# Two tile users regrouped by engine, the output projection's forms loaded in their stored layout, and its first half accumulated into the residual by transfers

## The chip, the cores and the metric

The kernel runs on one core of one Trainium2 chip. The metric is the device time of one execution in microseconds, the median of several executions. For the kernel before it is 2371.23 us (three runs, 2368.53 to 2372.38). Engines are called PE (TensorE, matmuls), DVE (VectorE), ACT (ScalarE), POOL (GpSimd, here mostly a queue that issues transfers) and SP (SyncE, a queue that issues transfers).

## The reference, cut to what matters

Two layers on a sequence of 512 tokens with 2048 features, all in 32-bit floats: forgetting attention (16 heads of 128), then retention (8 heads, keys of 256, values of 512). Each has one input projection, a gate, one output projection, a residual and a layer norm.

```python
def fox_branch(x, w_in, b_f, q_gain, k_gain, w_out):
    ...
    q = rms_norm(heads(q), q_gain)
    k = rms_norm(heads(k), k_gain)
    ...
    y = o * jax.nn.silu(gate)
    return jnp.einsum('bse,ed->bsd', y, w_out)

def retention_branch(x, w_in, w_out):
    ...
    o = group_norm_heads(o).reshape(B, S, RET_V_WIDTH).astype(gate.dtype)
    y = o * jax.nn.silu(gate)
    return jnp.einsum('bse,ed->bsd', y, w_out)

def reference(...):
    h = x
    for i in range(DEPTH):
        ...
        h = layer_norm(DEEPNORM_ALPHA * h + y, ln_gain[i], ln_bias[i])
    return h
```

The retention layer's output projection sums over 4096 features (8 heads of 512). The kernel does it in two halves of 2048 features, heads 0 to 3 and heads 4 to 7, whose results are added to the residual `DEEPNORM_ALPHA * h`.

## The kernel before, in words

**Matmuls.** A 32-bit product is made of three passes on split operands: every operand `t` is split into a rounded part `h` (ACT, L325) and the rest `l = t - h` (DVE, L326), and `mm3` issues `h*h`, `h*l` and `l*h` (L330, L331, L332). The large projections are `Unit`s, products of two 2x2 block matrices done with seven block products instead of eight (Strassen's way): each takes "forms" of the activations (`a11`, `a12`, `a22` and the sums `s1` to `s4`) and blocks of weights, some of which are sums too (`w_q`, DVE L595). The block results are combined in tiles called `kept` and in a buffer called `room`, and a finished quarter (m, n) of a unit's output goes to a function `sink`.

**Stages**, by the trace's lines: the first layer's projections and attention up to 835 us; its output projection with the layer norm and the transposes for the next layer from 835 to 1030 us; the eight retention heads up to about 2080 us; the second layer's output projection up to the end. That projection consists of units 14 and 15 (first four heads, left and right half of the output columns) and units 16 and 17 (last four heads).

**Order.** A planner (`Order`) writes the program block by block. Beside the matmul blocks there are tasks (Python generators); each `yield need(...)` names the DVE and ACT time that the next step costs, the buffers it takes and a condition, and the step is put into the program once the planner's debt of DVE and ACT leaves room. Each engine runs its instructions in the order written. SP issues the loads of weights, of stored forms (`y_raw`) and of the residual (`z_in`), in that one order; POOL issues the stores and the accumulating transfers. `tmp` is a ring of four buffers of 128x512, `mmp` a ring of two PSUM tiles for transposes and small products.

**What the change touches.**

- `to_parts` (L1099 to L1105), called 32 times between 144 and 799 us: it takes one `mmp` tile of transposed queries and keys, and for each of two pairs of columns ACT writes the scaled `qk_h` (L1102) and DVE the rest `qk_l` (L1103). Read and written by turns: ACT, DVE, ACT, DVE.
- `to_columns` (L1528 to L1592), the layer norm's transposes: sixteen times, PE transposes four 128x128 blocks into an `mmp` tile (L1567), and four copies with gain and bias bring them into a shared tile (called `raw` in the profile): j = 0 on ACT (L1585), j = 1 on DVE (L1583), j = 2 and 3 on ACT.
- `give_forms` (L842 to L846): when a retention head is done, ACT makes `y` and its negative `ny` (L1839, L1840) and POOL stores or accumulates them into the forms of the output projection in DRAM (`y_a` and `y_s` in the profile). The DRAM layout is 128 x 2 x 8 x 128. `given[1]` counts the heads so far.
- `fetch_forms` (L866 to L893): SP reads these forms back (L880) into `y_raw` in the layout 128 x 8 x 256, with a transfer for each of two halves of tokens and two halves of features, so a partition's row is four runs of 128 floats; then `split_form` splits them.
- `add_half` (L1890 to L1905), the sink of units 14 and 15: the residual's 16 blocks of 128x512 (`z_res`) are read back into the `tmp` ring by SP (`z_in`, L1474), DVE adds the finished quarter (L1898), and POOL stores the sum as `z_half` (L1899). Units 16 and 17 read `z_half` the same way.
- The tiles with finished quarters are freed by `done()`: (0,0), (0,1) and (1,1) lie in `kept` tiles or `room`, (1,0) still lies in PSUM (`acc`).

Of the kernel before, what the change touches and what calls it, by code (L numbers as in the profile page):

```python
# [11 lines left out]
F32 = mybir.dt.float32  # L12
# [5 lines left out]
P = 128  # L18
# [232 lines left out]
def trunk(ctx: ExitStack, tc: tile.TileContext, xq, x, fb_f, columns, wf_in, narrow, wide, ln_g, ln_b, rot, decay,  # L251
# [9 lines left out]
    def f32(t):  # L261
        return t.bitcast(F32)
# [571 lines left out]
           for f in (("a11", "a12", "a21", "a22") if i == 0 else FORM.values())} for i in range(3)]  # L834
    z_norm = [dram.tile([P, D], F32, name=f"z_norm{s}") for s in range(ST)]
    z_res = {(s, c): dram.tile([P, 512], F32, name=f"z_res{s}{c}") for s in range(ST) for c in range(4)}
    z_half = {(s, c): dram.tile([P, 512], F32, name=f"z_half{s}{c}") for s in range(ST) for c in range(4)}


    given = [0, 0]  # L840
# [25 lines left out]
    def fetch_forms(i, names):  # L866

        at = {}

        def loads():  # L870
            for n in names:
                if n not in VIA:
                    yield need(g0=1)
                    take("g0")
                t = pool.tile([P, 8, 256], F32, name="y_raw", tag=home[VIA[n]][0] if n in VIA else "g0")
                passing.add(VIA.get(n))
                for c in (0, 4):
                    yield need(wait=2, until=lambda: given[1] >= 4 * i)
                    for e in range(2):
                        nc.sync.dma_start(t[:, c:c + 4, e * P:(e + 1) * P], yf[i][n][:, e, c:c + 4])  # L880
                    at[n, c] = t, o.now

        spawn(loads(), 0)
        for n in names:
            for c in (0, 4):
                yield need(dve=1.14, act=0.97,
                           until=lambda: n not in passing and (n, c) in at and o.now - at[n, c][1] >= 4)
                if c == 0:
                    new_form(n)
                split_form(n, at[n, c][0][:, c:c + 4], c, c + 4)  # L890
            passing.discard(VIA.get(n))
            if n not in VIA:
                give("g0")  # L893
# [98 lines left out]
    class Pair:  # L992
# [88 lines left out]
        def normed(self):  # L1081

            yield need(until=lambda: self.have == 4 and fox["norms"] == self.i)
            raw = [self.raw[s // 2][:, s % 2] for s in range(ST)]
            r = self.ss
            yield need(dve=1.2)
            yield from rsqrt_steps(*[r.rearrange("p a b -> p (a b)")] * 2, 4 * ST, 1.0 / P, QK_EPS)
            scaled = {}
            for s in range(ST):
                yield need(dve=0.6, wait=0)  # L1090
                scaled[s] = o.due
                v = raw[s].rearrange("p (h d) -> p h d", h=4)
                nc.vector.tensor_mul(v, v, r[:, s, :, None].to_broadcast([P, 4, P]))
            yield need(until=lambda: all(free[t] for t in self.tags))
            for t in self.tags:
                take(t)
            self.qk = sb8("qk_h", self.tags[0], F32R), sb8("qk_l", self.tags[1], F32R)

            def to_parts(t, s):  # L1099
                for i, gain in ((0, gq), (2, gk)):  # L1100
                    h, l = (p[:, i:i + 2, s * P:(s + 1) * P] for p in self.qk)
                    nc.scalar.activation(h, t[:, i:i + 2], AF.Copy, scale=gain)  # L1102
                    nc.vector.scalar_tensor_tensor(l, t[:, i:i + 2], gain, f32(h), op0=ALU.mult, op1=ALU.subtract)  # L1103
                self.due = o.due
                give("mmp")  # L1105

            t, s, last = {}, ST if self.quick else 0, None
            for q in range(ST if self.quick else 0):
                yield need(act=0.75, dve=0.7, pe=0.45, wait=1 - q % 2, mmp=1, until=lambda: o.soon(scaled[q]))
                t[q] = by4(mmp())  # L1110
                for h in range(4):
                    nc.tensor.transpose(t[q][:, h], raw[q][:, h * P:(h + 1) * P], ident)
                to_parts(t[q], q)
            can = lambda: s < ST and free["mmp"] and o.soon(scaled[s])
            while s < ST or last is not None:
                yield need(act=0.75, dve=0.7, pe=0.45, until=lambda: last is not None or can())
                new = None
                if can():
                    new = s
                    t[s] = by4(mmp())  # L1120
                    for h in range(4):
                        nc.tensor.transpose(t[s][:, h], raw[s][:, h * P:(h + 1) * P], ident)
                    s += 1
                if last is not None:
                    to_parts(t[last], last)
                last = new
            give("in0")
            give("in1")
            fox["emptied"] = self.i + 1
            yield need()  # L1130
            fox["norms"] = self.i + 1
# [396 lines left out]
    def to_columns(m):  # L1528
# [28 lines left out]
        while i < 8 or last is not None or made:  # L1557
# [17 lines left out]
            if last is not None:  # L1575
                s, c = turns[last]
                es = slice(s % 2 * P, (s % 2 + 1) * P)
                d = aq[f"{m + 1}{c // 2 + 1}"][:, c % 2 * 4:c % 2 * 4 + 4, es]
                for j in range(4):
                    k = c * 4 + j  # L1580
                    g, b = cols[:, 2 + k:3 + k], cols[:, 2 + KT + k:3 + KT + k]
                    if j == 1:
                        nc.vector.tensor_scalar(d[:, j], ps[last][:, j], g, b, op0=ALU.mult, op1=ALU.add)  # L1583
                    else:
                        nc.scalar.activation(d[:, j], ps[last][:, j], AF.Identity, scale=g, bias=b)  # L1585
                give("mmp")
                if m == 0:
                    made.append(last)
                elif s % 2:
                    there.add((f"2{c // 2 + 1}", c % 2))  # L1590
# [296 lines left out]
                      then={**then, "p4": lambda h=h, last=last: (spawn(h.retain()), last())})  # L1887


    def add_half(u, held):  # L1890
        got, steps = loads_of(lambda s, c: z_res[s, c], u, "order", held)

        def sink(m, n, tile, done):
            def add():
                for e in range(2):
                    yield need(dve=0.6, until=lambda: (m, n, e) in got and o.now - got[m, n, e][1] >= 2)
                    t, _ = got.pop((m, n, e))
                    nc.vector.tensor_add(t, t, tile[:, e])  # L1898
                    nc.gpsimd.dma_start(z_half[2 * m + e, 2 * u + n], t)  # L1899
                    give("tmp", 3)  # L1900
                done()

            spawn(add(), 0)

        return sink, steps  # L1905

    sink, steps = add_half(0, 2)
    Unit(wide, 14, sink, u2="in1", p1="y0").run(then={"p6": lambda s=steps: spawn(s(), 1)})
    sink, steps = add_half(1, 2)
    Unit(wide, 15, sink, u2="k2").run(leaves=True, then={0: lambda s=steps: spawn(s(), 1), **fetch_while(2)})  # L1910

    gb = []

# [55 lines left out]
            else:  # L1969
                nc.gpsimd.dma_start(out[s * P:(s + 1) * P, cs], z, accum_op=ALU.add)  # L1970

    half = lambda s, c: z_half[s, c]
    spawn(join_room(), 0)
    sink, steps = add_z(0, 1, half, "order")
    Unit(wide, 16, sink, u2="k2").run(then={0: lambda s=steps: spawn(s(), 1)})
# [56 lines left out]
```

## Time and profile before

| | before |
|---|---|
| median of three runs | 2371.23 us |
| profiled execution, whole | 2373.73 us |
| its span from the first to the last instruction | 2372.0 us |
| mean granted TensorE clock | 0.993 |
| busy share of the span: PE, DVE, ACT, POOL | 97%, 80%, 51%, 7% |
| moved by transfers | 477.36 MB |

The span leaves out 1.73 us of the profiled execution. The busy share of PE is an average over stages; a table by stage, the waits and the transfers stand with the prediction. In rows that group instructions, the columns are: line, engine, operation, output and inputs, shapes, count, then busy time and mean ns of one, then the idle time of the engine just before them and what ended it.

### The profile page before, as it was taken

How to read it: one execution, taken by the hardware profiler on the slowest of the kernel's cores; microseconds unless marked ns; L12 is line 12 of the kernel's file. 1: busy time of each engine (PE TensorE's matmuls, PEld its weight loads, DVE VectorE, ACT ScalarE, POOL GpSimd, SP SyncE). 2: the span in 40 equal slices, each digit the busy share in tenths (PEclk: the TensorE clock that was granted, in tenths of full speed). 3: DMA queues.
4: the chain of work that ended last, by engine and by line, in shares of the span. 5: the costliest groups of instructions: out<-in, count | busy, mean ns of one | idle time of the engine just before them, and what ended most of it. 6: DMA issues, size and time to landing. Idle time of an engine off the chain costs nothing.

```text
span 2372.0 us, 32919 instructions
## 1 busy us (share of the span) xinstructions
PE 2307.9 (97%) x12424; PEld 1975.0 (83%) x12424; DVE 1892.5 (80%) x2477; ACT 1213.4 (51%) x1762; POOL 165.7 (7%) x256
## 2 busy tenths in 40 slices
PE   9999999999999999999999999999999999999995
PEld 9878778879899778888889898988888898787784
DVE  5887787787765656689889888888988889987877
ACT  4546556556555534565444545354545445554533
POOL 0000000000000000010100101010101000011002
PEclk9999999999999999999999999999999999999998
DMA  6356455455544456684685857575756659679778
GB/s 225 123 199 198 160 187 187 154 181 184 195 151 155 139 199 241 225 186 157 207 263 211 249 174 222 197 203 186 218 186 209 204 171 274 209 256 295 234 247 190
DMA packets 186350, 477.36 MB, mean 201 GB/s; under 512 B 18224, under 2 KB 63424, under 8 KB 185680
## 3 DMA queue, kind: packets, MB, share of 16 engines
q1 hardware_dynamic: 160288, 399.48, 50.3%
q0 software_dynamic: 25904, 75.78, 12.7%
q8 instruction: 97, 1.59, 0.3%
q14 instruction: 61, 0.50, 0.1%
HBM read 415.39 MB, written 64.00 MB: 202 GB/s over the span
## 4 chain that ended last, share of the span: by engine, by line
PE 62%; DVE 7%; DMA 4%; issue 3%; ACT 3%; POOL 0%; SPq 0%; DVEq 0%; ACTq 0%; POOLq 0%
PE acc L330 19%; PE acc L331 19%; PE acc L332 19%; DVE w_l L326 3%; DMA w_raw<-in_wide 2%; ACT w_h L325 2%; PE mmp L331 1%; PE mmp L330 1%; PE mmp L332 1%; PE mmp L1303 1%; DVE w_q L595 1%; DMA room<-in_wide 1%; PE mmp L1835 1%; PE mmp L1155 0%; DVE z L1936 0%
## 5 line engine op out<-in xcount | busy, mean ns | idle before, releaser
L325 ACT ACTIVATE w_h<-w_q 128x1024 fp32r<-128x1024 f32 x360 | 380.6, 1059 | 417.9 <-DVE w_q L595 221.6
L326 DVE TENSOR_TENSOR w_l<-w_raw,w_h 128x1024 fp32r<-128x1024 f32 x314 | 383.5, 1222 | 201.8 <-ACT w_h L325 200.5
L330 PE MATMUL acc<-w_h,a 128*128 128x512 f32 (+1 forms) x1440 | 536.5, 373 | 7.2 <-DVE kept L488 4.6
L331 PE MATMUL acc<-w_l,a 128*128 128x512 f32 (+1 forms) x1440 | 529.4, 368 | 3.1 <-DVE w_l L326 2.9
L332 PE MATMUL acc<-w_h,a 128*128 128x512 f32 (+1 forms) x1440 | 528.9, 367 | 0.0
L325 ACT ACTIVATE w_h<-w_raw 128x1024 fp32r<-128x1024 f32 x314 | 331.7, 1058 | 374.5 <-PE acc L332 181.0
L326 DVE TENSOR_TENSOR w_l<-w_q,w_h 128x1024 fp32r<-128x1024 f32 x360 | 439.2, 1221 | 100.3 <-ACT w_h L325 96.7
L331 PE MATMUL acc<-w_l,s 128*128 128x512 f32 (+1 forms) x1280 | 488.4, 382 | 10.7 <-DVE w_l L326 10.7
L330 PE MATMUL acc<-w_h,s 128*128 128x512 f32 (+1 forms) x1280 | 492.2, 385 | 1.6 <-ACT w_h L325 1.6
L332 PE MATMUL acc<-w_h,s 128*128 128x512 f32 (+1 forms) x1280 | 486.9, 380 | 0.0
L330 PEld LDWEIGHTS acc<-w_h,a 128*128 128x128 f32 x1440 | 272.5, 189 | 54.1 <-issue 8.5
L331 PEld LDWEIGHTS acc<-w_l,a 128*128 128x128 f32 x1440 | 272.8, 189 | 48.6 <-DVE w_l L326 7.5
L332 PEld LDWEIGHTS acc<-w_h,a 128*128 128x128 f32 x1440 | 272.3, 189 | 45.2
L331 PEld LDWEIGHTS acc<-w_l,s 128*128 128x128 f32 x1280 | 241.9, 189 | 60.0 <-DVE w_l L326 17.6
L332 PEld LDWEIGHTS acc<-w_h,s 128*128 128x128 f32 x1280 | 241.6, 189 | 45.8
L330 PEld LDWEIGHTS acc<-w_h,s 128*128 128x128 f32 x1280 | 241.6, 189 | 45.0 <-ACT w_h L325 2.0
L595 DVE TENSOR_TENSOR w_q<-w_q,w_raw 128x1024 f32<-128x1024 f32 x216 | 263.3, 1220 | 12.1 <-DMA w_raw<-in_wide 9.7
L332 PE MATMUL acc<-a,w_l 128*128 128x256 f32 x464 | 132.2, 285 | 1.7 <-DVE w_l L326 1.7
L330 PE MATMUL acc<-a,w_h 128*128 128x256 f32 x464 | 132.3, 285 | 1.5 <-ACT w_h L325 1.5
L331 PE MATMUL acc<-a,w_h 128*128 128x256 f32 x464 | 132.0, 285 | 0.0
L332 PE MATMUL acc<-s,w_l 128*128 128x256 f32 x448 | 126.8, 283 | 0.0
L331 PE MATMUL acc<-s,w_h 128*128 128x256 f32 x448 | 126.7, 283 | 0.0
(235 smaller groups left out, 2972.2 us busy)
## 6 DMA issues: line engine op xcount, KB each, us to landing
w_raw<-in_wide SPq DMA_DIRECT2D x364, 512.0 KB, 4.1
w_raw<-in_narrow SPq DMA_DIRECT2D x104, 512.0 KB, 3.7
w_q<-in_wide SPq DMA_DIRECT2D x72, 512.0 KB, 4.4
room<-in_wide SPq DMA_DIRECT2D x48, 512.0 KB, 4.5
y_s<-ny POOLq DMA_DIRECT2D x48, 256.0 KB, 7.1
y_s<-y POOLq DMA_DIRECT2D x40, 256.0 KB, 6.7
w_q<-in_narrow SPq DMA_DIRECT2D x18, 512.0 KB, 3.9
room<-in_narrow SPq DMA_DIRECT2D x18, 512.0 KB, 3.9
```

Source lines behind the costliest of these rows:

```text
L325: nc.scalar.activation(h, src, AF.Copy)
L326: nc.vector.tensor_sub(l, src, f32(h))
L330: nc.tensor.matmul(ps, a[0], b[0], start=start, stop=False, skip_group_check=True)
L331: nc.tensor.matmul(ps, a[0], b[1], start=False, stop=False, skip_group_check=True)
L332: nc.tensor.matmul(ps, a[1], b[0], start=False, stop=stop, skip_group_check=True)
L595: nc.vector.tensor_add(u.chain[c], u.chain[c], t)
L1303: nc.tensor.matmul(ps[:, k * P:], vh[:, k], pT[:, k, k * P:], start=k == 0, stop=k == ST - 1)
L1835: nc.tensor.transpose(ps[t - 1][:, i], g[t - 1][:, i * P:(i + 1) * P], ident)
```

## The change

1. `to_parts` issues both ACT writes of `qk_h` first, then both DVE writes of `qk_l`.
2. `to_columns` takes j in the order 0, 2, 3, 1: three ACT copies, then the DVE copy.
3. `fetch_forms` loads `y_raw` in the layout that DRAM has, 128 x 2 x 8 x 128, with one transfer for each half of the features (512 KB, runs of 512 floats) instead of two of 256 KB; the split reads and writes through rearranged views. 56 transfers become 28.
4. `add_half` no longer reads the residual, adds, and stores. POOL accumulates each finished block into `z_res` itself (DRAM), twelve straight from the tiles that hold them and four, those of quarter (1,0), from a copy `z_part` that ACT makes out of PSUM. Those from tiles are put into the program once the last head's forms are stored (`given[1] == RH`). `z_half` is gone; units 16 and 17 read `z_res`.

```diff
--- before.py
+++ after.py
@@ -834,7 +834,6 @@
            for f in (("a11", "a12", "a21", "a22") if i == 0 else FORM.values())} for i in range(3)]
     z_norm = [dram.tile([P, D], F32, name=f"z_norm{s}") for s in range(ST)]
     z_res = {(s, c): dram.tile([P, 512], F32, name=f"z_res{s}{c}") for s in range(ST) for c in range(4)}
-    z_half = {(s, c): dram.tile([P, 512], F32, name=f"z_half{s}{c}") for s in range(ST) for c in range(4)}
 
 
     given = [0, 0]
@@ -872,12 +871,11 @@
                 if n not in VIA:
                     yield need(g0=1)
                     take("g0")
-                t = pool.tile([P, 8, 256], F32, name="y_raw", tag=home[VIA[n]][0] if n in VIA else "g0")
+                t = pool.tile([P, 2, 8, P], F32, name="y_raw", tag=home[VIA[n]][0] if n in VIA else "g0")
                 passing.add(VIA.get(n))
                 for c in (0, 4):
                     yield need(wait=2, until=lambda: given[1] >= 4 * i)
-                    for e in range(2):
-                        nc.sync.dma_start(t[:, c:c + 4, e * P:(e + 1) * P], yf[i][n][:, e, c:c + 4])
+                    nc.sync.dma_start(t[:, :, c:c + 4], yf[i][n][:, :, c:c + 4])
                     at[n, c] = t, o.now
 
         spawn(loads(), 0)
@@ -887,7 +885,10 @@
                            until=lambda: n not in passing and (n, c) in at and o.now - at[n, c][1] >= 4)
                 if c == 0:
                     new_form(n)
-                split_form(n, at[n, c][0][:, c:c + 4], c, c + 4)
+
+                split(at[n, c][0][:, :, c:c + 4].rearrange("p e k t -> p k e t"),
+                      *(t[:, c:c + 4].rearrange("p k (e t) -> p k e t", e=2) for t in forms[n]))
+                ready[n].update(range(c, c + 4))
             passing.discard(VIA.get(n))
             if n not in VIA:
                 give("g0")
@@ -1097,10 +1098,13 @@
             self.qk = sb8("qk_h", self.tags[0], F32R), sb8("qk_l", self.tags[1], F32R)
 
             def to_parts(t, s):
-                for i, gain in ((0, gq), (2, gk)):
-                    h, l = (p[:, i:i + 2, s * P:(s + 1) * P] for p in self.qk)
-                    nc.scalar.activation(h, t[:, i:i + 2], AF.Copy, scale=gain)
-                    nc.vector.scalar_tensor_tensor(l, t[:, i:i + 2], gain, f32(h), op0=ALU.mult, op1=ALU.subtract)
+
+                parts = [(gain, t[:, i:i + 2], *(p[:, i:i + 2, s * P:(s + 1) * P] for p in self.qk))
+                         for i, gain in ((0, gq), (2, gk))]
+                for gain, x, h, _ in parts:
+                    nc.scalar.activation(h, x, AF.Copy, scale=gain)
+                for gain, x, h, l in parts:
+                    nc.vector.scalar_tensor_tensor(l, x, gain, f32(h), op0=ALU.mult, op1=ALU.subtract)
                 self.due = o.due
                 give("mmp")
 
@@ -1576,7 +1580,7 @@
                 s, c = turns[last]
                 es = slice(s % 2 * P, (s % 2 + 1) * P)
                 d = aq[f"{m + 1}{c // 2 + 1}"][:, c % 2 * 4:c % 2 * 4 + 4, es]
-                for j in range(4):
+                for j in (0, 2, 3, 1):
                     k = c * 4 + j
                     g, b = cols[:, 2 + k:3 + k], cols[:, 2 + KT + k:3 + KT + k]
                     if j == 1:
@@ -1887,27 +1891,30 @@
                       then={**then, "p4": lambda h=h, last=last: (spawn(h.retain()), last())})
 
 
-    def add_half(u, held):
-        got, steps = loads_of(lambda s, c: z_res[s, c], u, "order", held)
+    def add_half(u):
 
         def sink(m, n, tile, done):
             def add():
                 for e in range(2):
-                    yield need(dve=0.6, until=lambda: (m, n, e) in got and o.now - got[m, n, e][1] >= 2)
-                    t, _ = got.pop((m, n, e))
-                    nc.vector.tensor_add(t, t, tile[:, e])
-                    nc.gpsimd.dma_start(z_half[2 * m + e, 2 * u + n], t)
-                    give("tmp", 3)
-                done()
+                    to = z_res[2 * m + e, 2 * u + n]
+                    if (m, n) == (1, 0):
+
+                        yield need(act=0.5, tmp=1)
+                        t = tmp("z_part")
+                        nc.scalar.activation(t, tile[:, e], AF.Copy)
+                        nc.gpsimd.dma_start(to, t, accum_op=ALU.add)
+                        give("tmp", 4)
+                    else:
+                        yield need(until=lambda: given[1] == RH)
+                        nc.gpsimd.dma_start(to, tile[:, e], accum_op=ALU.add)
+                done(0 if (m, n) == (1, 0) else 4)
 
             spawn(add(), 0)
 
-        return sink, steps
-
-    sink, steps = add_half(0, 2)
-    Unit(wide, 14, sink, u2="in1", p1="y0").run(then={"p6": lambda s=steps: spawn(s(), 1)})
-    sink, steps = add_half(1, 2)
-    Unit(wide, 15, sink, u2="k2").run(leaves=True, then={0: lambda s=steps: spawn(s(), 1), **fetch_while(2)})
+        return sink
+
+    Unit(wide, 14, add_half(0), u2="in1", p1="y0").run()
+    Unit(wide, 15, add_half(1), u2="k2").run(leaves=True, then=fetch_while(2))
 
     gb = []
 
@@ -1969,7 +1976,7 @@
             else:
                 nc.gpsimd.dma_start(out[s * P:(s + 1) * P, cs], z, accum_op=ALU.add)
 
-    half = lambda s, c: z_half[s, c]
+    half = lambda s, c: z_res[s, c]
     spawn(join_room(), 0)
     sink, steps = add_z(0, 1, half, "order")
     Unit(wide, 16, sink, u2="k2").run(then={0: lambda s=steps: spawn(s(), 1)})
```

What this does to the order of instructions, at three places:

ACT in `to_columns`, around two of the sixteen turns, with what each instruction waits for (before):

```order
L325 ACTIVATE w_h<-w_raw 128x1024 [waits DMAHW0_49,PE_49]
L1585 ACTIVATE raw<-mmp,cols 128x128 [waits PE_49]
L1585 ACTIVATE raw<-mmp,cols 128x128 [waits DVE_49]
L1585 ACTIVATE raw<-mmp,cols 128x128
L325 ACTIVATE w_h<-w_q 128x1024 [waits DMAHW1_49,PE_49]
```

and of the change:

```order
L325 ACTIVATE w_h<-w_raw 128x1024 [waits DMAHW0_49,PE_49]
L1589 ACTIVATE raw<-mmp,cols 128x128 [waits PE_49]
L1589 ACTIVATE raw<-mmp,cols 128x128 x2
L325 ACTIVATE w_h<-w_q 128x1024 [waits DMAHW1_49,PE_49]
L1589 ACTIVATE raw<-mmp,cols 128x128 [waits PE_49]
```

The wait for DVE at the second copy of a turn is gone. On DVE the copy of the turn, which waited for PE alone, now waits for PE and for ACT's last copy; in `to_parts` the same holds for the first of the two DVE writes, and the second waits for nothing.

ACT in the last head's end, while units 14 and 15 run. L1839/L1840 (L1843/L1844 of the change) make `y` and `ny`; L1849 (L1853) scales a tile with the group norm's factor ahead of its transpose; `a` is a split of a loaded form. Before:

```order
L325 ACTIVATE a_18791<-y_raw 128x1024
L325 ACTIVATE w_h<-w_q 128x1024
L1849 ACTIVATE kept<-kept,gn_r 128x512
L325 ACTIVATE w_h<-w_raw 128x1024
L325 ACTIVATE w_h<-w_q 128x1024
L325 ACTIVATE w_h<-room 128x1024
L325 ACTIVATE a_18791<-y_raw 128x1024
L325 ACTIVATE w_h<-w_q 128x1024
L325 ACTIVATE w_h<-w_raw 128x1024
L325 ACTIVATE w_h<-w_q 128x1024 x2
L1839 ACTIVATE y<-mmp 128x512
L1840 ACTIVATE ny<-mmp 128x512
```

and of the change:

```order
L325 ACTIVATE a_18757<-y_raw 128x1024
L325 ACTIVATE w_h<-w_q 128x1024
L1853 ACTIVATE kept<-kept,gn_r 128x512
L325 ACTIVATE w_h<-w_raw 128x1024
L1843 ACTIVATE y<-mmp 128x512
L1844 ACTIVATE ny<-mmp 128x512
L1853 ACTIVATE gate<-gate,gn_r 128x512
L325 ACTIVATE w_h<-w_q 128x1024
L1843 ACTIVATE y<-mmp 128x512
L1844 ACTIVATE ny<-mmp 128x512
L1853 ACTIVATE gate<-gate,gn_r 128x512
L325 ACTIVATE a_18757<-y_raw 128x1024
```

The first `y` and `ny` come six instructions earlier, and the second pair follows four rows behind the first; before, the other three of the last head's four turns come after this piece. The same goes for POOL, which issues the transfers of `y` and `ny` and those of the sums. POOL's rows before, from the last stores of the residual on (numbers are those of DRAM tiles: `y_a_138`, `y_s_139` and the like are forms of the second half, `z_half_164` and so on the sums):

```order
L1869 DMA z_res_159<-z_in 128x512
L1869 DMA z_res_163<-z_in 128x512
L1899 DMA z_half_165<-z_in 128x512
L1899 DMA z_half_169<-z_in 128x512
L1899 DMA z_half_173<-z_in 128x512
L1899 DMA z_half_177<-z_in 128x512
L846 DMA y_a_138<-y 128x512
L846 DMA y_s_139<-y 128x512
L1899 DMA z_half_164<-z_in 128x512
L1899 DMA z_half_168<-z_in 128x512
L1899 DMA z_half_172<-z_in 128x512
L1899 DMA z_half_176<-z_in 128x512
```

and of the change, where the residual's tiles are `z_res_148` and on:

```order
L845 DMA y_a_140<-y 128x512
L845 DMA y_s_141<-ny 128x512
L845 DMA y_s_142<-ny 128x512
L845 DMA y_s_139<-ny 128x512
L1909 DMA z_res_149<-kept 128x512
L1909 DMA z_res_157<-kept 128x512
L1909 DMA z_res_153<-kept 128x512
L1909 DMA z_res_161<-kept 128x512
L1909 DMA z_res_148<-room 128x512
L1909 DMA z_res_152<-room 128x512
L1905 DMA z_res_156<-z_part 128x512
L1905 DMA z_res_160<-z_part 128x512
```

All twelve transfers of the last head's `y` and `ny` (four of them shown) now stand together, and behind them stand accumulations into `z_res` in one row, the first six from `kept` and `room`. Before, the stores of sums lay between the forms' transfers. On SP, the 16 loads `z_in<-z_res` among the weights of units 14 and 15 are gone, and each pair of `y_raw` loads is one.

## The prediction

> **What bounds the kernel now.** First the page's opening rows, then the table by stage.
>
> ```profile
> span 2372.0 us, 32919 instructions
> PE 2307.9 (97%) x12424; PEld 1975.0 (83%) x12424; DVE 1892.5 (80%) x2477; ACT 1213.4 (51%) x1762; POOL 165.7 (7%) x256
> core 0: us, PE busy (x) PEld busy (x) DVE busy (x) ACT busy (x) POOL busy (x), PEclk, DMA share, GB/s
> 140.00:175.00 35.00, 33.26 (x152) 26.09 (x150) 30.11 (x38) 17.73 (x23) 1.06 (x2) 1.00 0.56 206
> 725.00:800.00 75.00, 72.32 (x470) 64.34 (x470) 42.55 (x95) 41.53 (x100) 0.00 (x0) 1.00 0.39 130
> 935.00:1030.00 95.00, 88.58 (x509) 74.86 (x508) 57.02 (x82) 57.84 (x93) 5.86 (x9) 0.98 0.67 215
> 1030.00:2000.00 970.00, 968.76 (x5547) 852.96 (x5547) 851.29 (x1040) 478.92 (x548) 90.08 (x131) 1.00 0.67 208
> 2000.00:2100.00 100.00, 97.64 (x427) 78.79 (x426) 92.71 (x115) 50.90 (x53) 3.30 (x6) 1.00 0.73 236
> 2145.00:2240.00 95.00, 88.82 (x377) 70.83 (x375) 79.20 (x72) 49.21 (x50) 8.02 (x13) 0.98 0.87 279
> ```
>
> PE is the bound: busy for 2307.9 of 2372.0 us, and over the 970 us of the retention heads for all but 1.24. The change takes no matmul away, so it can win only what PE loses where it touches the order: 1.7 us in 140 to 175, 2.7 in 725 to 800 (both `to_parts`), 6.4 in 935 to 1030 (`to_columns`), 2.4 in 2000 to 2100 and 6.2 in 2145 to 2240 (the output projection). Two of these rows have a clock under 1.00. Narrow windows at those places and at two others show why:
>
> ```profile
> 969.00:975.00 6.00, 4.97 (x26) 4.76 (x27) 5.71 (x7) 2.79 (x5) 0.00 (x0) 0.72 0.31 99
> 2164.00:2170.00 6.00, 3.94 (x11) 3.16 (x12) 5.93 (x6) 1.06 (x1) 0.57 (x1) 0.72 0.99 312
> 2083.00:2089.00 6.00, 4.79 (x21) 4.00 (x22) 5.93 (x7) 2.76 (x3) 0.90 (x2) 1.00 0.82 270
> 852.00:858.00 6.00, 4.70 (x21) 3.93 (x22) 3.56 (x5) 1.75 (x2) 0.00 (x0) 1.00 0.67 237
> ```
>
> In the first two the clock's mean is 0.72: 0.28 x 6 = 1.7 us of PE's work lost, apart from the gap itself. In the last two PE also idles (6 - 4.79 = 1.2 and 6 - 4.70 = 1.3 us) and keeps its clock. Where a gap of some 2 us goes, then, 1.7 us of half-speed matmuls can go with it. The gaps, grouped by the waiting matmul, in the stages 725 to 800 (two rows), 935 to 1030 (four), 2000 to 2100 (two) and 2145 to 2240 (three):
>
> ```profile
> L1112 PE MATMUL mmp<-ident,qk_raw 128*128 128x128 f32 x32 | 4.4, 274 | 1.7 <-DVE qk_l L1103 1.7
> L330 PE MATMUL mmp<-qk_h 128*128 128x256 f32 (+2 forms) x9 | 3.4, 374 | 0.9 <-ACT qk_h L1102 0.9
> ...
> L331 PE MATMUL acc<-w_l,a 128*128 128x512 f32 x72 | 28.4, 395 | 0.9 <-DVE w_l L326 0.9
> L330 PE MATMUL acc<-a,w_h 128*128 128x256 f32 x76 | 22.6, 297 | 1.5 <-ACT w_h L325 1.5
> L332 PE MATMUL acc<-a,w_l 128*128 128x256 f32 x76 | 22.4, 294 | 1.7 <-DVE w_l L326 1.7
> L1567 PE MATMUL mmp<-ident,z 128*128 128x128 f32 x64 | 10.0, 279 | 2.3 <-ACT raw L1585 2.3
> ...
> L330 PE MATMUL acc<-w_h,a 128*128 128x512 f32 x67 | 26.3, 392 | 1.3 <-DVE kept L488 1.3
> L331 PE MATMUL acc<-w_l,s 128*128 128x512 f32 x64 | 25.5, 399 | 1.0 <-DVE w_l L326 1.0
> ...
> L331 PE MATMUL acc<-w_l,s 128*128 128x512 f32 x77 | 30.4, 395 | 2.8 <-DVE w_l L326 2.8
> L330 PE MATMUL acc<-w_h,a 128*128 128x512 f32 x48 | 19.7, 410 | 2.6 <-DVE kept L488 2.5 <-ACT w_h L325 0.2
> L331 PE MATMUL acc<-w_l,a 128*128 128x512 f32 x48 | 19.4, 405 | 0.8 <-DVE w_l L326 0.8
> ```
>
> **`to_parts`.** What ACT and DVE wait for at its two lines:
>
> ```profile
> L1102 ACT ACTIVATE qk_h<-mmp,cols x64: 452/473/478, 144.0 to 798.1; 128x256 fp32r<-128x256 f32 x64
>   DVE qk_l L1103: 49.3, 32
> L1103 DVE SCALAR_TENSOR_TENSOR qk_l<-mmp,cols,qk_h x64: 474/483/486, 146.5 to 798.6; 128x256 fp32r<-128x256 f32 x64
>   ACT qk_h L1102: 27.7, 36
> ```
>
> In each of 32 calls ACT's second write waits for DVE's first (49.3 / 32 = 1.54 us) and DVE's second for ACT's second. The four run one after the other: 2 x 0.473 + 2 x 0.483 = 1.9 us and the hand-overs. Changed, ACT does both at once and is free for the next `w_h`; DVE begins one ACT write later (0.47) and then runs both through. ACT gains up to 49.3 us that it mostly doesn't need, since PE was waiting for it in few places. Two of those are this chain's own (1.7 and 0.9 in 725 to 800), and the 1.7 us in 140 to 175 follow a `w_l` behind it. Bounds: 0 to 4.3. I take **3**: the first two whole less the 0.47 by which DVE's first write comes later, and half of the third.
>
> **`to_columns`.**
>
> ```profile
> L1585 ACT ACTIVATE raw<-mmp,cols x48: 439/452/459, 936.2 to 1022.0; 128x128 f32<-128x128 f32 x48
>   DVE raw L1583: 22.4, 16
> ```
>
> In each of 16 turns ACT waits 22.4 / 16 = 1.40 us inside the turn, with the next `w_h` queued behind it; DVE's copy stands behind whatever `w_l` (1.22 us) it has in hand. After the change ACT's turn is three copies in a row, and DVE's copy frees the `mmp` tile last. All four gaps of this stage hang on ACT being held: 2.3 directly, 1.5 on the `w_h` behind, 1.7 + 0.9 on the `w_l` that needs that `w_h`; together 6.4, and the 1.7 of the clock at 969 makes 8.1. DVE is busy for 57.02 of 95 us here, so it can carry a wait of its own: two ACT copies (2 x 0.45) for each of 16 turns is 14 us of its 38 idle. I keep 1 us for turns in which the tile now comes free later: **7**, bounds 4 (only the two direct terms 2.3 + 1.7) and 8.1.
>
> **The output projection.** Its loss is 2.3 + 6.2 of gaps and 1.7 of clock at 2164, in all 10.2. Three edits bear on it together.
>
> ```profile
> L1898 DVE TENSOR_TENSOR z_in<-z_in,kept x10: 679/684/686, 2082.2 to 2192.3; 128x512 f32<-128x512 f32 x10
> L1898 DVE TENSOR_TENSOR z_in<-z_in,acc x4: 680/680/681, 2115.5 to 2201.3; 128x512 f32<-128x512 f32 x4
> L880 SPq DMA_DIRECT2D y_raw<-y_s x32: 383/498/4801, 1975.9 to 2200.3; - x32
> L1840 ACT ACTIVATE ny<-mmp 128x512 f32<-128x512 f32 x4 | 2.4, 599 | 4.3 <-DMA y_s<-ny 2.7 <-DMA y_s<-y 0.8 <-issue 0.7
> y_s<-ny POOLq DMA_DIRECT2D x48, 256.0 KB, 7.1
> 2124.98 0.58 ACT L1839 ACTIVATE y<-mmp 128x512 f32<-128x512 f32 x1
> 2126.54 1.04 ACT L443 ACTIVATE kept<-acc 128x1024 f32<-128x1024 f32 x1
> q1 hardware_dynamic: 10224, 33.30, 49.9%
> q1 hardware_dynamic: 5271, 5.67, 79.4%
> q0 software_dynamic: 649, 1.43, 49.9%
> ```
>
> (The last three rows are queues by packets, MB and share of 16 engines: the loads in 1300 to 1500, the loads in 2143 to 2165, POOL's transfers in 2126 to 2143.)
>
> *DVE.* 16 adds of 0.68 go, 10.9 us in a stretch where DVE is at 93% (2000 to 2100) and 83%. Four ACT copies come (0.58, as `y<-mmp` of the same size; 2.3 us on an engine at 51%). A `kept` combination that PE waits for (1.3 and 2.5 us) came behind one such add each: 1.4 goes.
>
> *Loads.* In 2143 to 2165 the transfer engines are all but full. The plain loads of 1300 to 1500 cost 0.499 x 16 x 200 / 33.30 = 48 engine-us for a MB; the mixture with short `y_raw` runs 0.794 x 16 x 22 / 5.67 = 49. Longer runs save next to nothing in the engines; 28 fewer issues save 28 x 0.5 = 14 us of SP's queue, and the one that took 4.8 us goes where its forms are ready before.
>
> The Trainium skill ("DMA: Bandwidth & Descriptors", section Specifications) gives 512 bytes as the least transfer for full line rate; `y_raw`'s runs are 128 floats, just 512 bytes. By it the edit of the layout gains nothing in the engines, and 49 against 48 agrees.
>
> *The order.* The last `y` ran at 2124.98; its row in the changed order stands among blocks that ran before at some 2085 to 2093. It and the transfers behind it come some 35 us earlier or more, so the accumulations no longer meet the `y_raw` and weight loads of 2143 to 2165. In their place stand 16 accumulations into `z_res`, most in one burst with them. A POOL transfer costs 0.499 x 17 us / (1.43 / 0.262) = 1.56 us of all engines; 12 + 6 in the burst are 28 us in some 35 to 45 us, beside loads that take half of the engines (49.9%). That just fits, and weights come late where it doesn't: between 0 and 13 us of transfers, hidden by weights loaded ahead; I take 1 us lost.
>
> Sum: 1.4 (DVE), 1.7 (the clock at 2164, as its gap of 2.5 loses 0.68 to under 2), half of the `w_l` gaps, 0.5 x (1.0 + 2.8 + 0.8) = 2.3, and 0.6 for the issue that waits; less 1 for the burst: **5**. Bounds: 10.2 gained, 3 lost (a `w_raw` late once by what `w_l` waited for at most, 2.8).
>
> **Sum.** 3 + 7 + 5 = 15. The profiled execution took 2373.73 (1.73 around its span), so 2358.7; the median of the three runs is 2.5 lower, and the same saving from 2371.23 gives **2356**.
>
> **The rivals.**
>
> 1. *The burst eats the third term.* The engines at 0.99 in 2164 to 2170 show what the queue looks like when full. Then only 3 + 7: 2361. Chance 0.20.
> 2. *The waits only change sides.* DVE now waits for ACT's last copy, and at 2083 and 2164 DVE is busy 5.93 of 6 us. If `mmp` tiles come free as late as before, `to_parts` gives 1, `to_columns` 2, the projection between 0 and 5: 2363 to 2368, say 2366. Against it: DVE's 38 idle us in 935 to 1030. Chance 0.14.
> 3. *Slower: the accumulations hold a buffer.* Before, DVE freed unit 14's tiles; now a tile is free when POOL's transfer out of it has landed, and the 12 + 6 are one queue. ACT's copy into a reused tile at 2126.5 needs them. If sixteen of them must land from 2081 on, where the second `y` of the change would run, it holds from (2126.5 - 2081) / 16 = 2.8 us apiece. At 1.56 (engines alone) it doesn't. At 4.3, midway to the 7.1 to landing, the tile is free at 2150; ACT is held 23.5 us, less two blocks of weights split ahead (2 x 2.9), and PE loses 17.7 + 1.7 of clock = 19.4. With 10 gained before: 2371.2 + 9.4 = 2380. Landings overlap in the trace (1.43 MB, five transfers, in 17 us, 3.1 apart, while POOL had no more to issue), so the chance is 0.07.
> 4. *The clock doesn't follow the gaps.* Then both dips stay, 3.4 of the 15: 2360. Chance 0.06. The Trainium skill ("TensorE: Matmul & The Clock Gate", section HAM oscillation) warns of idle gaps over some 3.4 us; the gaps at the two dips are no longer than 2.5 us, so the measurement speaks against that bound.
> 5. *Nothing is gained,* as the order moved but the last waits didn't: 2371. Chance 0.03; the first copies have lost their wait in the order.
>
> **How the numbers follow.** Forecast 0.50, rivals 0.20, 0.14, 0.07, 0.06, 0.03. A measurement of this kernel can tell about 0.2%, 4.7 us, from no change: below 2366.5 is faster. Faster: 0.50 + 0.20 + 0.06 and half of rival 2 = 0.83; same 0.10; slower 0.07. Range: all bounds at their best, 4.3 + 8.1 + 10.2 = 22.6, give 2348.6, with half of the runs' spread, 1.9, 2347; upward, 2364 if the projection alone loses 3, and 2367 takes in most of rival 2. Left out are rivals 3 and 5, and the tails, some 0.17.
>
> **What would show it.** Right: no wait for DVE before the second copies (49.3 and 22.4 us gone) and PE busy for over 94 of 95 us in 935 to 1030; a clock of 1.00 at 971 and 2166; L1898 gone and its `kept` gaps with it; `ny` on ACT waiting no more for `y_s`. Wrong: gaps in 2085 to 2130 on `w_l` with weights landing late (rival 1), `kept<-acc` on ACT waiting for a `z_res` transfer (rival 3), ACT or DVE idle as long as before with the other engine's name (rival 2).

## The result, and the profile after

The changed kernel takes 2341.81 us (median of three runs, 2341.23 to 2342.85) against 2371.23: 29.4 us less, ratio 0.9879 with a 95% interval of 0.9856 to 0.9901. A repetition in another session gave 2342.64 against 2370.79 (0.9878, 0.9864 to 0.9893). The forecast was 15 us less and a range of 2347 to 2367: right in sign and mostly in place, but half the size, and the result lies outside the range.

The opening rows of its page (profiled execution 2341.23 us):

```profile
span 2339.4 us, 32843 instructions
PE 2293.9 (98%) x12424; PEld 1971.9 (84%) x12424; DVE 1881.4 (80%) x2461; ACT 1213.0 (52%) x1766; POOL 170.9 (7%) x256
```

The span is 32.6 us shorter, and PE does the same 12424 matmuls in 14.0 us less *busy* time (2307.9 to 2293.9). That second number is the key to the error: less than 19 of the 32.6 us stood in idle columns. Of the other 14.0, some 6 are the clock: before's first profile has half-clock stretches (the granted clock is 0.50 there) at 258, 971, 2166 and 2323 us, each worth some 1.5 us, which this one hasn't. The rest, some 8, was lost without showing as idle time (p2 below has an example).

Next the table by stage. Its ends lie at the same matmuls as those of before (the counts of PE are equal but in the fifth row, into which the last head's transposes have moved), so lengths can be subtracted. Rows: 140 to 175, 175 to 725, 725 to 800, 935 to 1030, 2000 to 2100 and 2145 to 2240 us of before. Columns as before: length, then busy time of PE, PEld, DVE, ACT, POOL, the clock, the share of the transfer engines, GB/s.

```profile
140.06:172.43 32.37, 32.37 (x152) 26.34 (x150) 29.85 (x38) 17.74 (x23) 1.06 (x2) 1.00 0.59 220
172.43:717.03 544.60, 537.27 (x2873) 455.00 (x2873) 420.75 (x637) 317.81 (x647) 24.98 (x44) 1.00 0.54 181
717.03:788.75 71.72, 71.32 (x470) 64.54 (x470) 43.01 (x97) 41.44 (x100) 0.00 (x0) 1.00 0.41 135
923.57:1007.45 83.88, 83.88 (x509) 74.33 (x508) 58.92 (x84) 58.83 (x95) 5.87 (x9) 1.00 0.77 249
1977.22:2077.48 100.26, 98.97 (x439) 80.07 (x438) 90.49 (x111) 55.42 (x62) 7.85 (x11) 1.00 0.68 223
2121.10:2207.35 86.25, 85.93 (x377) 70.04 (x375) 73.29 (x63) 47.88 (x49) 8.11 (x10) 1.00 0.83 262
```

The differences: 2.6, 5.4 and 3.3 us in the three stretches of the first stage (11.3), 11.1 in `to_columns`, 8.7 in 2145 to 2240. PE is busy without a gap in 140 to 172 and in 924 to 1007. The stretch 175 to 725, for which nothing was forecast, gave more than either of the two stretches that were named for `to_parts`; some 1.5 of its 5.4 us are the clock at 258.

The waits inside the two regrouped functions, as each line's view tells (what its engine waited for, us and times):

```profile
L1105 ACT ACTIVATE qk_h<-mmp,cols x64: 452/466/487, 144.1 to 785.4; 128x256 fp32r<-128x256 f32 x64
  PE mmp L1116: 14.9, 5
L1107 DVE SCALAR_TENSOR_TENSOR qk_l<-mmp,cols,qk_h x64: 473/477/485, 146.6 to 786.5; 128x256 fp32r<-128x256 f32 x64
  ACT qk_h L1105: 12.6, 5
```

ACT's 49.3 us of waits for DVE are gone, and DVE's waits for ACT fell from 27.7 to 12.6 us. The three ACT copies of `to_columns` (L1589) and DVE's (L1587) waited for nothing at all.

### The profile page after: what moved, and what is told of

Same layout as the page of the kernel before. It is cut to its first block, busy times and chain, and to the rows that moved or that the text cites. A ratio compares the mean times of both kernels' runs of the same rounds, so it can differ in the third digit from the quotient of the medians.

```text
span 2339.4 us, 32843 instructions
## 1 busy us (share of the span) xinstructions
PE 2293.9 (98%) x12424; PEld 1971.9 (84%) x12424; DVE 1881.4 (80%) x2461; ACT 1213.0 (52%) x1766; POOL 170.9 (7%) x256
## 4 chain that ended last, share of the span: by engine, by line
PE 80%; DVE 10%; DMA 4%; ACT 3%; issue 2%; SPq 0%; DVEq 0%; ACTq 0%; POOLq 0%
PE acc L330 24%; PE acc L331 24%; PE acc L332 24%; DVE w_l L326 4%; DMA w_raw<-in_wide 2%; ACT w_h L325 2%; DVE w_q L595 2%; PE mmp L332 2%; PE mmp L330 2%; PE mmp L331 2%; PE mmp L1307 1%; DMA v_sum<-in_wide 1%; PE mmp L1159 1%; DVE w_raw L590 1%; DMA room<-in_wide 1%
```

## Experiments

Each kernel was timed against the kernel before on the same chip. The kernel before gave medians of 2371.18 (p1 to p4), 2370.79 (p5 to p7, p0) and 2371.36 (p8 to p10). Beside the time, the start of each of the 10992 large matmuls was subtracted from that of the same matmul in before's profile; that difference, followed along the kernel, is called the shift below.

| | median, us | ratio to before, 95% interval |
|---|---|---|
| p1, `to_parts` alone | 2359.80 | 0.9957, 0.9942 to 0.9972 |
| p2, `to_columns` alone | 2359.62 | 0.9957, 0.9941 to 0.9973 |
| p3, layout of `y_raw` alone | 2369.49 | 0.9993, 0.9983 to 1.0003 |
| p4, `add_half` alone | 2363.84 | 0.9969, 0.9960 to 0.9979 |
| p5, `to_parts` in two pairs of eight | 2368.84 | 0.9989, 0.9980 to 0.9999 |
| p6, order of the last head alone | 2368.09 | 0.9985, 0.9975 to 0.9994 |
| p7, change without the condition `given[1] == RH` | 2347.78 | 0.9900, 0.9885 to 0.9914 |
| p0, the change again | 2342.64 | 0.9878, 0.9864 to 0.9893 |
| p8, change, all `to_columns` copies on ACT | 2342.99 | 0.9882, 0.9868 to 0.9897 |
| p9, change without `to_parts` | 2354.56 | 0.9929, 0.9912 to 0.9945 |
| p10, layout and order | 2367.76 | 0.9986, 0.9976 to 0.9995 |

### The four edits one by one

p1, in short:

```diff
-for i, gain in ((0, gq), (2, gk)):
-    ACT h <- t; DVE l <- t, h
+for gain, x, h, _ in parts:
+    ACT h <- x
+for gain, x, h, l in parts:
+    DVE l <- x, h
```

> Before with the regrouped to_parts alone. Theory (each part pays in its own stage, and a stall costs its gap plus the overlap that consecutive matmuls lose, which the idle columns leave out): matmuls up to 835 us come 9 to 11 us earlier at the end of that stretch, of them 6 at the calls themselves (165 to 172, 736, 795 to 800) and 3 at later attention steps (320 to 336, 505 to 515); nothing changes behind 835; time 9 to 11 us shorter. Rival (the idle columns are the whole loss, the rest of the 11 us seen in the changed kernel came from somewhere else): 3 us shorter.

It took 11.4 us less, and the shift at 800 us is 9.8. The same three stretches, ends at the same matmuls:

```profile
140.10:172.45 32.35, 32.35 (x151) 26.33 (x150) 29.84 (x38) 17.75 (x23) 1.06 (x2) 1.00 0.60 221
172.45:718.60 546.15, 538.72 (x2873) 456.11 (x2873) 420.65 (x637) 317.93 (x647) 24.98 (x44) 1.00 0.55 180
718.60:790.16 71.56, 71.16 (x470) 64.39 (x470) 42.82 (x97) 41.28 (x100) 0.00 (x0) 1.00 0.41 136
```

2.65, 3.85 and 3.44 us: the theory's 6 at the calls, and somewhat more than its 3 behind them; the time is a little over its 9 to 11. The changed kernel's further 1.5 us in the middle stretch is a half-clock stretch that before and p1 have near 255 us and its profile has not (last section). The count of 151 for 152 in the first row is one matmul at the edge.

p2:

```diff
-for j in range(4):
+for j in (0, 2, 3, 1):
```

> Before with the order 0, 2, 3, 1 in to_columns alone. Theory: 10 to 11 us shorter, all between 935 and 1030 us, PE without a gap there and no half-clock stretch at 971. Rival (idle columns are the whole loss): 6 to 8 us shorter. Rival (the wait moves to DVE): 2 us shorter with DVE idle before its copy.

11.6 us less, a little over the theory's 10 to 11; the shift grows by 11.1 between 935 and 1030:

```profile
934.44:1018.30 83.86, 83.86 (x509) 74.29 (x508) 58.90 (x84) 58.91 (x95) 5.88 (x9) 1.00 0.77 249
```

Before, 509 matmuls took 95.00 us with PE busy for 88.58. Now they take 83.86 and PE is busy all of them. Of the 11.14 us, 6.42 had been idle; 4.72 had been counted as busy. Where those were is seen at a single gap of before, in its timeline (start, duration, engine, line, form, idle time before it):

```profile
1020.45 0.39 PE L332 MATMUL acc<-w_h,a 128*128 128x512 f32 x1
1020.68 0.39 PE L330 MATMUL acc<-w_h,a 128*128 128x512 f32 x1
1021.38 0.50 PE L331 MATMUL acc<-w_l,a 128*128 128x512 f32 x1 [0.31 <-DVE w_l L326]
1021.72 0.40 PE L332 MATMUL acc<-w_h,a 128*128 128x512 f32 x1
1021.95 0.39 PE L330 MATMUL acc<-w_h,a 128*128 128x512 f32 x1
```

A matmul lasts 0.39 us but the next one starts after 0.23, since they overlap. Across the gap the starts are 0.70 apart, then 0.34: 0.47 + 0.11 = 0.58 us lost, where the idle column says 0.31. A stall under 0.16 us (0.39 - 0.23) shows no idle at all. Taken as start-to-start times against the median of the same form, the stage lost 7.9 us at nine gaps (6.4 idle), 3.6 without a gap and 1.5 at half clock, 13.0 in all. p2 keeps 1.8 of it, all without a gap, so what went is 7.9 + 1.8 = 9.7 and the clock's 1.5.

p3 loads `y_raw` as 128 x 2 x 8 x 128:

```diff
...
-for e in range(2):
-    nc.sync.dma_start(t[:, c:c + 4, e * P:(e + 1) * P], yf[i][n][:, e, c:c + 4])
+nc.sync.dma_start(t[:, :, c:c + 4], yf[i][n][:, :, c:c + 4])
...
```

> Before with the new layout of the y_raw loads alone, 28 loads instead of 56. Theory (engine cost per MB is the same, only SP issues are saved): 0 to 2 us shorter, the gap of 2.5 us at 2166 stays. Rival (the short runs are what fills the transfer engines in 2143 to 2165): 5 us or more shorter, and that gap goes.

1.7 us less, and the interval includes none. The time is as the theory had it, but the gap at 2166 is 1.0 us in its profile, where the theory had 2.5 staying (rows below).

p4 replaces `add_half`:

```diff
...
-    nc.vector.tensor_add(t, t, tile[:, e])
-    nc.gpsimd.dma_start(z_half[2 * m + e, 2 * u + n], t)
...
+    yield need(until=lambda: given[1] == RH)
+    nc.gpsimd.dma_start(to, tile[:, e], accum_op=ALU.add)
...
```

> Before with add_half by accumulating transfers alone. Theory (DVE's adds and the late y and ny of the last head are what holds the projection): 7 to 9 us shorter, all behind 2080 us, the half-clock stretch at 2166 gone. Rival (it needs the faster y_raw loads too): under 4 us shorter, with w_l gaps left at 2145 to 2240.

7.3 us less, as the theory had it; its profile has no half-clock stretch near 2166. Its shift moves only behind 2080, but for turns of 1.5 us that come with half-clock stretches and at 1230, where several profiles differ though their code there is the same.

### Why the first stage gave more than its calls

> Before with to_parts regrouped in two of its eight pairs of heads alone, those whose calls run at 270 to 284 and at 460 to 471 us, where PE has no gap. Theory (DVE and ACT carry what they lose in a call into the attention steps behind it, where PE waits for DVE's row sums): the gap at 506 shrinks by 1.1 us and the one at 320 by 0.4, so 1.5 to 2.5 us shorter up to 835 us, and nothing changes at 165, 735 and 795. Rival (a call pays only where it stands): no change in those places, 0 to 0.5 us shorter.

```diff
...
+for some in ((parts,) if self.i in (1, 3) else (parts[:1], parts[1:])):
...
```

2.0 us less (0.2 to 4.7 by the interval). In the profile only the gap at 506 moved, by 1.1 us; the group of that matmul in 498 to 512 us, in before:

```profile
L1303 PE MATMUL mmp<-pT,by_head 128*128 128x512 f32 (+3 forms) x8 | 2.4, 446 | 1.5 <-DVE sm L1206 1.5
```

and in p5:

```profile
L1306 PE MATMUL mmp<-pT,by_head 128*128 128x512 f32 (+3 forms) x8 | 2.4, 446 | 0.4 <-DVE sm L1209 0.4
```

The regrouped calls run at 460 to 471, where PE lost nothing. The pay-off comes some 35 us later. From 480.5 us of before on, DVE runs without idle time up to these row sums; between the calls and there it still waits, in before 1.9 us for a load into `w_raw`, in p5 1.5 us for such loads and 1.4 for ACT's `w_h`; SP issues these loads when a `w_l` of DVE's is done. How the lateness passes through these waits isn't followed step by step; p5 shows that it does. The second place that the theory named, 320, kept its 1.5 us: that half of the expectation was a miss. With all pairs regrouped (p1) the shift there is 0.4; through which calls stays open. Over 175 to 725, the gaps before the matmuls that wait for row sums fell from 3.0 to 1.5 us in p1 and those before L1314's (L1317 in p1) from 1.4 to 0.1; p5 explains the first kind alone.

### What in the projection does it

> Before with one residual block held in the tmp ring instead of two (add_half(u, 1)), so that three of the last head's four pairs of y and ny go out early, while the 16 loads, DVE adds and stores stay. Theory (the early y and ny are the larger part of what add_half gives): 4 to 6 us shorter, the gap of 2.5 us at 2166 gone or under 1 us. Rival (the DVE adds are it): 0 to 2 us shorter, the gap stays over 2 us.

```diff
-sink, steps = add_half(0, 2)
+sink, steps = add_half(0, 1)
-sink, steps = add_half(1, 2)
+sink, steps = add_half(1, 1)
```

> Before with the new y_raw layout and one residual block held in the tmp ring instead of two: three of four pairs of y and ny early, fewer loads issued, while the residual's loads, the 16 DVE adds and the stores stay. Theory (the stall around 2166 is one, and either edit takes it away; the adds on DVE are the rest of add_half's gain): 3 to 5 us shorter than before, that is 4 to 6 less than layout and accumulation together. Rival (the order and the layout are all of it): 7 to 9 us shorter.

(p10 has p3's diff and p6's.) p6 is 2.7 us shorter, p10 3.6. PE's group with the wait for the `kept` combination near 2166, in the stretch that answers to 2145 to 2240; the prediction has its row in before (2.5 us). First in a second profile of before (b0, below):

```profile
L330 PE MATMUL acc<-w_h,a 128*128 128x512 f32 x48 | 18.8, 391 | 1.6 <-DVE kept L488 1.6
```

in p1, p2 and p5, whose code for the projection is that of before:

```profile
L330 PE MATMUL acc<-w_h,a 128*128 128x512 f32 x48 | 19.3, 402 | 2.4 <-DVE kept L488 2.4
L330 PE MATMUL acc<-w_h,a 128*128 128x512 f32 x48 | 19.6, 407 | 2.4 <-DVE kept L488 2.4
L330 PE MATMUL acc<-w_h,a 128*128 128x512 f32 x48 | 19.5, 406 | 2.0 <-DVE kept L488 2.0
```

in p3:

```profile
L330 PE MATMUL acc<-w_h,a 128*128 128x512 f32 x48 | 18.8, 392 | 1.0 <-DVE kept L488 1.0
```

in p6:

```profile
L330 PE MATMUL acc<-w_h,a 128*128 128x512 f32 x48 | 18.8, 391 | 0.2 <-DVE kept L488 0.2
```

and in p10 0.3 us. In p4 and the changed kernel the wait is gone.

It is one stall: the earlier `y` and `ny` take it away, all but 0.2 or 0.3 us, with DVE's adds still there. p3's 1.0 lies under all five profiles with the old order and layout (1.6 to 2.5), but as these differ by 0.9 among themselves, one profile doesn't settle that the layout shrinks it. A stall goes only once: by the medians p3 and p4 give 1.7 + 7.3 = 9.0, while the ratios of p9 and p2 (0.9929 / 0.9957) leave 6.6 us for both together; with these intervals the difference itself isn't shown. p6's time missed its theory (4 to 6) though its gap did as the theory said, and p10, whose theory said 3 to 5, hit. Taking the adds off DVE, or the loads and stores that go with them, is the rest; the two were not separated.

> The changed kernel without the condition that the accumulations from tiles wait for the last head (given[1] == RH): four of the sixteen then stand on POOL ahead of the last head's y and ny. Theory (their place matters little, the engines have room): within 2 us of the changed kernel. Rival (accumulations ahead of y and ny delay the forms of the second half): 3 to 6 us longer than the changed kernel, with gaps in 2110 to 2210.

```diff
-yield need(until=lambda: given[1] == RH)
+yield need()
```

> The changed kernel once more, as the companion of the run without the condition: 2341 to 2343 us. By both theories its matmuls come 22 to 23 us earlier than before's by 1050 us and 32 to 33 by 2345, as in its first profile, give or take 1.6 us for each half-clock stretch that falls in one profile and not in the other.

p0 took 2342.64 us, as expected. Without the condition the kernel takes 5.1 us longer than p0, as the rival said. The two intervals still overlap (0.9885 to 0.9914, 0.9864 to 0.9893), but the trace has the cause. The groups of the last head's copies on ACT in 2040 to 2100 us of p7:

```profile
L1844 ACT ACTIVATE ny<-mmp 128x512 f32<-128x512 f32 x4 | 2.4, 590 | 4.9 <-DMA y_s<-y 4.9
L1843 ACT ACTIVATE y<-mmp 128x512 f32<-128x512 f32 x4 | 2.3, 584 | 2.2 <-DMA y_s<-y 2.2
```

that of `ny` in p0, where `y` waits for nothing:

```profile
L1844 ACT ACTIVATE ny<-mmp 128x512 f32<-128x512 f32 x4 | 2.4, 592 | 0.4 <-DMA y_s<-y 0.4
```

and PE's new gap in p7, in 2060 to 2100 us:

```profile
L330 PE MATMUL acc<-w_h,a 128*128 128x512 f32 x40 | 16.0, 401 | 2.1 <-ACT w_h L325 1.9 <-DVE kept L488 0.2
```

Three accumulations of the residual ahead of the first `y_s<-y` on POOL, and a fourth ahead of the second, delay it; ACT's next `y` and `ny` wait for its buffer, the next `w_h` stands behind them, and PE waits. From 2080 to 2300 us of before, the matmuls of p7 take 213.6 us and those of p0 210.5; the rest of the 5.1 isn't located. The queue's order, not the work, is what the condition buys.

### Repetition, a cross-check and an attempt at more

> The kernel before once more, for a second profile of it. Theory (the stalls in 935 to 1030 and in the calls of to_parts are set by the order, those at 2145 to 2170 hang on when transfers land and differ from one execution to the next): the gaps of the first two within 0.3 us of the first profile; the 2.5 us at 2166 different by a microsecond or more. Rival (all of them are set by the order): 2.5 us there again. Half-clock stretches may fall elsewhere, 1.5 us each.

The gaps at the calls and in `to_columns` were there again within 0.2 us. Both half-clock stretches on which the forecast had counted, at 971 and at 2166, were not, and the gap at 2166 was 1.6 instead of 2.5: 0.9 apart, where the theory had a microsecond or more. The shift between the two profiles is 3.9 us at that place alone (this second execution took 2374.68 us in all). It is b0 that is the exception at 2166: p1, p2 and p5, with the same code there, have gaps of 2.4, 2.4 and 2.0 and a half-clock stretch each.

So the edits are best judged over all profiles, each stretch between the same matmuls. From the start to 835 us of before took 833.3 to 838.5 us in the eight with the old `to_parts` (mean 835.58) and 823.6 to 825.2 in the five with the new (824.44): 11.1 less. From 935 to 1030 took 93.8 to 95.0 in the eight with the old `to_columns` (94.26) and 83.84 in each of the six with the new: 10.4 less. From 2145 to 2240 took 90.8 to 95.0 in the five with the old projection (93.1) and 86.1 to 87.7 in the four with layout, accumulation and condition (86.6): 6.5 less.

> The changed kernel without the regrouped to_parts (the other three edits in). Theory (the edits pay apart from one another, what stands before 835 us is settled there): 10 to 12 us longer than the changed kernel, all of it before 835 us. Rival (part of what to_parts gave alone is given by the others too): under 8 us longer.

2354.56: by the ratios to before, 0.9929 - 0.9878 = 0.51%, 12 us longer than the change, as the theory had it.

p8, in short:

```diff
-if j == 1:
-    nc.vector.tensor_scalar(d[:, j], ps[last][:, j], g, b, op0=ALU.mult, op1=ALU.add)
-else:
-    nc.scalar.activation(...)
+nc.scalar.activation(...)
```

> The changed kernel with all four copies of a to_columns turn on ACT, none on DVE. Theory (what held PE was that ACT waited inside the turn, not its work): 0 to 1 us from the changed kernel, PE still without a gap in 923 to 1008, ACT 16 x 0.45 = 7 us busier there. Rival (ACT is nearly the bound there, at 59 of 85 us busy): gaps on w_h come back, 2 us or more longer.

2342.99, no different from the change, and PE has no gap in 923 to 1008. ACT is 4.5 us busier there (63.9 against 59.4), where the theory had 7. The waits, not ACT's work, were what it cost; nothing is gained further either. No kernel tried beats the changed one.

## Why the prediction was wrong in size

**What bounds the kernel: right as a place, wrong as a measure.** All savings came out of the stages named, or a stretch between two of them. But "the change can win only what PE loses" was followed by idle columns as that loss. That is one of two steps that failed: in `to_columns` 6.4 us of gaps were 9.7 us of lost starts that the edit took away, beside the clock's 1.5. The other is the list of places where `to_parts` could pay, and it cost more.

**`to_parts`, forecast 3 (0 to 4.3), measured 11.4 (9.8 of shift up to 800 us).** The largest error. Its own stretches gave 2.65 + 3.44 = 6.1 instead of 3: 4.0 of gaps and 2.1 around them. And "PE was waiting for it in few places" left out 175 to 725, which the prediction's table has no row for and which gave 3.85. Of that, 3.05 did stand in the idle column (10.5 us idle in before, 7.4 in p1); part of it (the gap at 506) comes by lateness that is carried out of a call over 35 us, as p5 shows. The bound of 4.3 was no bound, as it held only one kind of loss in two of three stretches.

**`to_columns`, forecast 7 (4 to 8.1), measured 11.6 (11.1 of shift, 10.4 by the means).** Mechanism right: all four gaps hung on ACT being held, and DVE's copy waited for nothing in its new place. Of the 4.1 us of shift missing, some 3.2 are the losses that no idle column shows; the 1 us kept back for later `mmp` tiles wasn't needed. The 1.7 for the clock was not to be counted on: with the old order, p1 and p3 have a half-clock stretch there too, b0, p4, p5, p6 and p10 have none.

**The output projection, forecast 5 (-3 to 10.2), measured 29.4 - 11.4 - 11.6 = 6.4, or 6.6 by p9 and p2.** Near in size, in part by luck. The reasons held in part: early `y` and `ny` and the order of POOL's queue mattered (p6, p7), longer runs little (p3). The terms were off in both directions. The forecast took 1.4 of the 3.8 us of `kept` gaps and half of the 4.6 of `w_l` gaps; in the changed kernel 0.2 of the one and 1.4 of the other are left. Gaps were undercounted again as well: 2145 to 2240 alone became 8.7 us shorter in the profile, clock included. Against that, the first profile of before was long there, 95.0 against 93.1 in the mean. The changed kernel also has a new gap near the end; here PE's group in 2300 to 2313:

```profile
L331 PE MATMUL acc<-w_l,a 128*128 128x512 f32 x11 | 4.4, 399 | 1.7 <-DVE w_l L326 1.7
```

In the first profile of before the same stretch has no gap; p0 and p8 have one of 2.7 and 2.8 there. DVE does the last layer norm's row factors ahead of that `w_l`, while ACT has made its `w_h`. It costs nothing that can be seen in the whole: from the matmul at 2300 of before to the last instruction, before's two profiles take 72.0 and 74.6 us and those of the changed kernel 72.1 and 71.9 (p0).

**The rivals.** The burst (1) and the held buffer (3) did not come in the change; p7 shows how near their relatives are: 5 us for four transfers ahead of the forms. The waits did not change sides (2). The clock (4) lies between: it follows gaps, but not each time.

**What would show it** did: the waits of 49.3 and 22.4 us gone, L1898 gone with all but 0.2 us of its `kept` gaps, PE busy all 83.9 us of the stage, the clock 1.00 at both places; ACT's `ny` still waits 0.4 us for `y_s` in p0, not none.

## What to carry to other kernels

What a stall costs an engine that overlaps its instructions is read from start-to-start times against their median, not from idle columns: in one stage here the columns held 6.4 of 9.7 us. When two engines write by turns into one tile, group the writes by engine, and look for the pay-off on each engine's chain behind the call, not at the call alone. Before counting on a clock stretch or a gap that hangs on transfers, take several profiles: here the first two disagreed, and it was the second that was the exception at 2166.

## What the runs showed of the hardware

Half-clock stretches lie on a fixed grid of 3.41 us, and a gap's place on it decides: within each of the 14 profiles, all changes of the clock lie whole multiples of 3.413 us apart. Two windows of that grid around the gap of 2.4 us near 255 (columns as in the table by stage), in before:

```profile
254.40:257.81 3.41, 1.04 (x9) 0.80 (x8) 3.38 (x5) 1.43 (x2) 0.00 (x0) 1.00 0.28 77
257.81:261.23 3.42, 3.42 (x10) 2.64 (x10) 3.42 (x4) 1.50 (x3) 0.00 (x0) 0.50 0.99 319
```

in the first profile of the changed kernel:

```profile
250.60:254.01 3.41, 1.68 (x10) 1.19 (x8) 3.38 (x5) 0.84 (x1) 0.00 (x0) 1.00 0.00 0
254.01:257.43 3.42, 2.77 (x14) 2.34 (x15) 3.42 (x4) 2.09 (x5) 0.00 (x0) 1.00 0.94 299
```

and in its second (p0):

```profile
250.65:254.06 3.41, 1.17 (x8) 0.77 (x6) 3.38 (x5) 1.36 (x2) 0.00 (x0) 1.00 0.17 29
254.06:257.48 3.42, 3.29 (x10) 2.72 (x11) 3.42 (x4) 1.57 (x4) 0.00 (x0) 0.50 0.98 281
```

PE idles 3.41 - 1.04 = 2.37 us in before's first window and the next one has half the clock. In the changed kernel's first profile the grid cuts the same gap in two (3.41 - 1.68 = 1.73, and the rest in the next window), and the clock stays; in its second, 2.24 us fall into one window, and it halves. Over the 14 profiles of this study, between 20 and 2300 us, each of the 27 full-clock windows with 1.95 us of idle or more is followed by one at half clock, and none with 1.88 or less. The grid lies differently against the kernel's start in each execution, so a gap of 2.4 us costs 1.5 us more in some executions and nothing in others. The Trainium skill ("TensorE: Matmul & The Clock Gate", section HAM oscillation) warns of gaps over some 3.4 us; here under 2 us of idle in one window are enough, and the measurement decides.
